# Down projection of a transformer block: six instead of five feature blocks by seven products, other homes for two operand sets, another order of blocks

## The chip, the core and the metric

The kernel runs on one core of a Trainium2 chip. Its time is the device time of one execution in microseconds. Before the change it takes 769.16 us (median of 3 runs, 768.88 to 769.38).

## The reference

One layer of an encoder: a token mixer (two attention groups), cross-attention into 256 memory tokens, and a SwiGLU feed-forward network, each between two RMS norms, on 512 tokens of width 1024, all in float32. The change lies in the last product, `@ w_down`, of the feed-forward network:

```python
D_MODEL = 1024
SEQ = 512
D_FF = -(-8 * D_MODEL // 768) * 256          # 2816

def swiglu(h, w_gate_up, w_down):
    g, u = jnp.split(h @ w_gate_up, 2, axis=-1)
    return (jax.nn.silu(g) * u) @ w_down

    ...
    h = rms_norm(x, g_ffn_pre[l])
    x = x + rms_norm(swiglu(h, w_gate_up[l], w_down[l]), g_ffn_post[l])
```

## The kernel before

Every float32 operand is held as two parts, a rounded high part and the remainder as a low part, and a product is three matmuls: high by high, high by low, low by high (`mm3`, lines 143, 144 and 146). ScalarE (ACT) makes the high part by a cast, VectorE (DVE) the low part by a subtraction. So each new operand costs both engines a pass.

**The down projection.** The hidden layer has 2816 features, 11 blocks (0 to 10) of 256. The output is made in two halves of 512 columns. For each half the loop at the end of the kernel goes through the feature blocks in the order of `DOWN[half]` and adds each block's product into the four accumulators of the half, one for each tile of 128 tokens. The last two blocks of half 0, and the last three of half 1, are `ends`: they are taken tile by tile, so that a tile is ready before the next one begins.

A *plain* block is 4 tiles x 2 x 3 = 24 matmuls of 512 columns (`down`). The blocks in `SEVEN` are computed by Winograd's form of Strassen's method instead: tokens, features and columns are each split in two, and the 2 x 2 by 2 x 2 block product takes seven products of half size instead of eight (`seven_products`). That is 7 x 2 x 3 = 42 matmuls of 256 columns. Four of the products go to banks of their own (p1, p5, p6, p7) that sum over all such blocks, and `gather` adds them up behind the last one.

A seven-product block needs two things that a plain one doesn't:

- An *operand set* of the hidden features: seven pieces of 128 x 256, four of them the blocks themselves and three made of sums, each as a high and a low part. `late_seven(u)` makes the set of block u: ACT casts pieces of 256, 512 and 1024 columns, and DVE subtracts as many and makes four sums of 256 (lines 1306 to 1309). The set is made once, in half 0, and used in both halves. Its home is two buffers, one for the high and one for the low parts: "latex" for blocks 4 and 5 (tags x1 and x2), "latehi" and "latelo" for 6 and 7.
- Weights of which four 256-column pieces are sums. `seven_down` makes them as two entries of the ring: a first one of three pieces as they are (lines 1001 and 1002, 256 and 512 columns), then three sums on DVE (lines 1007 to 1009, 512, 256 and 256 columns) and a second entry of 1024 columns (lines 922 and 923).

**The weight ring** has four places of 1024 columns, for high and low parts. A plain block takes one place, a seven-product block two. `take` starts as many fills as places are free; a place is free when PE has done with the entry four earlier. The raw weights come by DMA from the SyncE queue into three buffers (`fraw`), each of which is loaded again when DVE has subtracted from it for the last time.

**When the sets are made.** While half 0 works on blocks 0, 1, 2 and 3 (all plain), the sets of 4, 5, 6 and 7 are made. Behind block 4's products those of the last two stored blocks follow: block 9 is split whole into a high and a low part (`late`, for a plain product) in the buffer "latev" (tag vm), and block 8, copied first to "f8", gets a set in what is left of "latev" and in "latep" (tag pt). The buffers of tags vm and pt held the hidden blocks 1 to 7 and 8 to 9 until then, so they come free with the last reader of those.

Here the order on each engine is set by a scheduler from the program order and its priorities; each engine then works strictly in that order.

Of the kernel before, what the change touches and what calls it, by code (L numbers as in the profile page):

```python
# [8 lines left out]
F32 = mybir.dt.float32  # L9
F32R = mybir.dt.float32r  # L10
AF = mybir.ActivationFunctionType
ALU = mybir.AluOpType
AX = mybir.AxisListType

P = 128
# [17 lines left out]
AS_WEIGHTS, AS_MOVING = 16, 48  # L33
# [3 lines left out]
def hybrid_block_kernel(  # L37
# [20 lines left out]
    act, dve, pool, pe = nc.scalar, nc.vector, nc.gpsimd, nc.tensor  # L58
# [12 lines left out]
    def f32(ap):  # L71
        return ap.bitcast(F32)
# [119 lines left out]
    def bcast(g):  # L192
        return bass.AP(g.tensor, g.offset, [[0, P], [1, D]])
# [11 lines left out]
    for side in range(2):  # L205
        for g in fox_order if side == 0 else (0, 1):
            c = (0, 1544)[side] + 256 * g
            n = 264 if (side, g) == (0, 1) else 256
# [20 lines left out]
    ox = ctx.enter_context(tc.tile_pool(name="ox", bufs=1))  # L229

    with tc.tile_pool(name="mix", bufs=1, reuse_waits="tile") as bp:
# [126 lines left out]
        for t in range(NT):  # L358
# [3 lines left out]
                out=z[:, t, :], in0=acc0[t][:, 256:264], scalar=r, in1=gn[:, B_F : B_F + 8],  # L362
# [34 lines left out]
        for b in range(3):  # L397
            l = bp.tile([P, 2, SEQ], F32R, tag=f"L{b}", name=f"L{b}")
# [209 lines left out]
        for n, (side, g) in enumerate(order):  # L608
            with later(-20):
                q, kt, kl, v = group_proj(f"{side}{g}")  # L610
            if n == 3:
# [4 lines left out]
                for k in range(0, KB, 2):  # L616
                    b = msq[:, 2 * (k > 0) : 2 * (k > 0) + 2, :]
# [44 lines left out]
    with tc.tile_pool(name="cross", bufs=1, reuse_waits="tile") as cp:  # L662
        vm = cp.tile([P, 2 * 2 * D + 64], F32R, tag="vm", name="vm")
        vm = vm[:, : 2 * 2 * D].rearrange("p (s t n) -> p s t n", s=2, t=2)
        pt = cp.tile([P, 2 * 2 * SEQ + 64], F32R, tag="pt", name="pt")
        pt = pt[:, : 2 * 2 * SEQ].rearrange("p (s k n) -> p s k n", s=2, k=2)
# [16 lines left out]
        with later(-115):  # L683
            for c in range(4):
                hi, lo = unit()
                acc = bank("a")
                for b in range(2):
# [9 lines left out]
                    out=kT[:, 1, 2 * c : 2 * c + 2, :], in0=a3,  # L697
                    in1=f32(kT[:, 0, 2 * c : 2 * c + 2, :]), op=ALU.subtract,
# [7 lines left out]
        for half in range(2):  # L706
            hi, lo = unit()
            for t in range(NT):
                acc = bank("a")
                for k in range(4):  # L710
# [5 lines left out]
                    out=m, in0=acc, scalar=rs_g[1][:, t : t + 1], in1=m, op0=ALU.mult, op1=ALU.add  # L716
# [3 lines left out]
                if half:  # L720
                    r = small(1, "prs")
                    dve.scalar_tensor_tensor(
                        out=r, in0=mix_ms[:, 0, t : t + 1], scalar=EPS, in1=mix_ms[:, 1, t : t + 1],
# [4 lines left out]
                        out=mix[:, t, :], in0=mix[:, t, :], scalar=r, in1=xo[t], op0=ALU.mult, op1=ALU.add  # L728
# [39 lines left out]
        for h in range(4):  # L768
            hi, lo = unit()
            q = qq[:, h % 2]  # L770
            for b in range(2):
                acc = bank("a")
                cs = slice(b * P, (b + 1) * P)
                for k in range(KB):
# [3 lines left out]
                    out=q[:, 1, b, :], in0=acc, scalar=1.0 / 16.0, in1=f32(q[:, 0, b, :]),  # L778
                    op0=ALU.mult, op1=ALU.subtract,
                )  # L780
            p = cp.tile([P, NT, NMEM], F32, tag="xp", name=f"xp{h}", bufs=2)
            for i in range(0, NT, 2):
                s = bank("s")
                for j in range(2):
# [8 lines left out]
                    out=nm, in_=s.rearrange("p (j n) -> p j n", j=2), axis=AX.X, op=ALU.max, negate=True  # L793
# [9 lines left out]
                for j in range(2):  # L803
                    dve.tensor_scalar(
                        out=p[:, i + j, :], in0=p[:, i + j, :], scalar1=rs[:, j : j + 1],
# [11 lines left out]
            for b in range(2):  # L817
                acc = bank("o")
                cs = slice((2 * h + b) * P, (2 * h + b + 1) * P)
                for k in range(2):  # L820
# [6 lines left out]
                    out=oTl[2 * h + b], in0=acc, in1=f32(oTh[2 * h + b]), op=ALU.subtract  # L827
# [150 lines left out]
        def item(at, size, fill):  # L978
            items.append((at, at + size, fill))

        SEVEN = (4, 5, 6, 7, 8)
        DOWN = ((0, 1, 2, 3, 4, 5, 6, 7, 8, 9, 10), (0, 4, 5, 6, 7, 8, 1, 2, 3, 9, 10))
        dslot = [0]

        def down_slot():
            dslot[0] += 1
            return 1024 * ((dslot[0] - 1) % 4)
# [27 lines left out]
        for half in range(2):  # L1015
            for i in DOWN[half]:
                if i in SEVEN:
                    seven_down(i, half)
                    continue
                at = down_slot()  # L1020
# [33 lines left out]
        gh, gl, gf = {}, {}, []  # L1054
# [31 lines left out]
        gf_views = {}  # L1086
# [24 lines left out]
        for pair in range(2):  # L1111
            ns = slice(pair * 256, (pair + 1) * 256)
# [173 lines left out]
        def room(p, tag, n, bufs=1):  # L1286
            t = p.tile([P, n + 16], F32R, tag=tag, name=f"late{tag}", bufs=bufs)
            return t[:, 16 : 16 + n].rearrange("p (c n) -> p c n", n=256)

        x1, x2 = (room(ox, tag, 14 * 256) for tag in ("x1", "x2"))  # L1290
        late7 = [(x1[:, 0:7], x1[:, 7:14]), (x2[:, 0:7], x2[:, 7:14])]
        late7 += [tuple(room(wp, tag, 7 * 256, 2) for _ in range(2)) for tag in ("hi", "lo")]
        late7 = dict(zip(SEVEN, late7))

        def late_seven(u):

            h, l = late7[u]
            f = gf_views[u].rearrange("p (c n) -> p c n", n=256)

            def put(d, a):  # L1300
                act.copy(h[:, d], f[:, a])
                dve.tensor_tensor(out=l[:, d], in0=f[:, a], in1=f32(h[:, d]), op=ALU.subtract)

            put(slice(0, 1), slice(0, 1))
            put(slice(1, 3), slice(2, 4))
            dve.tensor_tensor(out=f[:, 3], in0=f[:, 1], in1=f[:, 3], op=ALU.add)
            dve.tensor_tensor(out=f[:, 1], in0=f[:, 0], in1=f[:, 1], op=ALU.subtract)
            dve.tensor_tensor(out=f[:, 0], in0=f[:, 3], in1=f[:, 0], op=ALU.subtract)
            dve.tensor_tensor(out=f[:, 2], in0=f[:, 2], in1=f[:, 0], op=ALU.subtract)
            put(slice(3, 7), slice(0, 4))  # L1310

        def late(u, flat):
            h, l = (flat[:, i * 1024 : (i + 1) * 1024] for i in range(2))
            act.copy(h, gf_views[u])
            dve.tensor_tensor(out=l, in0=gf_views[u], in1=f32(h), op=ALU.subtract)
            for b in range(2):
                gh[2 * u + b] = h[:, b * 512 : (b + 1) * 512]
                gl[2 * u + b] = l[:, b * 512 : (b + 1) * 512]

        yd = big.tile([P, NT, D], F32, tag="sB", name="yd")  # L1320

# [11 lines left out]
        for half, tail in enumerate((2, 3)):  # L1333
# [31 lines left out]
            def block(dst, u, a, w, c, end=False):  # L1365
                for n in range(2):
                    to = slice(n * 256, (n + 1) * 256)
                    b = dst
                    if isinstance(dst, tuple):
                        b, to = accs[dst[0] + n], (left, right)[dst[1]]  # L1370
                    lhs = [x[:, a, n * P : (n + 1) * P] for x in late7[u]]
                    mm(b, to, lhs, (w[0][:, c], w[1][:, c]), end and n == 1)

            def seven_products(u, last):
# [21 lines left out]

            body = DOWN[half][: FB // 2 - tail]
            for i in body:
                if i in SEVEN:
                    if half == 0 and i == SEVEN[0]:  # L1400
                        cuts.append(P)
                    seven_products(i, i == SEVEN[-1])
                    if half == 0 and i == SEVEN[0]:
                        spare = cp.tile([P, 4160], F32R, tag="vm", name="latev")
                        copied = cp.tile([P, 1024], F32, tag="xp", name="f8", bufs=2)
                        act.copy(copied, gf_views[8])
                        gf_views[8] = copied
                        late(9, spare)
                        at = 2048 + AS_WEIGHTS
                        lows = cp.tile([P, 2112], F32R, tag="pt", name="latep")[:, AS_WEIGHTS:]  # L1410
                        late7[8] = tuple(
                            a.rearrange("p (c n) -> p c n", n=256) for a in (spare[:, at : at + 1792], lows[:, :1792])
                        )
                        late_seven(8)
                        gb3 = cp.tile([P, D], F32, tag="xp", name="gb3", bufs=2)
                        spare3 = cp.tile([P, D], F32, tag="xp", name="spare3", bufs=2)
                        junk3, gained = spare3[:, :512], spare3[:, 512:]
                        nc.gpsimd.dma_start(gb3, bcast(g_ffn_post))
                    if i == SEVEN[-1]:
                        gather()  # L1420
                    continue
                (w,) = take()
                if half == 0 and i < 4:
                    late_seven(SEVEN[i])
                for t in range(NT):
                    if half and t == NT - 1 and DOWN[1].index(i) + 1 == DOWN[1].index(SEVEN[0]):
                        cuts.append(384)
                    down(t, i, w, half == 1 and t == NT - 1 and i == body[-1])
                    if held and t == 1:
                        cur.p3()  # L1430
                        held.clear()
                        cur.op2()
                        cur.mult(0)
                        keep(cur.u, cur.dst)
            ends = take(tail)
            for t in range(NT):
                yt = yd[:, t, cs]
                if half and t == NT - 1:
# [3 lines left out]
                    for n, (to, b) in enumerate(((left, bank("a")), (right, bank("a")))):  # L1442
                        for j, w in enumerate(ends):
                            down(t, DOWN[half][FB // 2 - tail + j], w, j == tail - 1, (to,), b)
                        dve.tensor_tensor(out=yt[:, to], in0=b[:, to], in1=yt[:, to], op=ALU.add)
# [7 lines left out]
                for j, w in enumerate(ends):  # L1453
                    down(t, DOWN[half][FB // 2 - tail + j], w, j == tail - 1)
                if half == 0:
# [68 lines left out]
```

## Time and profile before

| | before |
|---|---|
| median of 3 runs | 769.16 us |
| the profiled execution | 769.24 us, of which the profile's span is 767.5 us |
| instructions | 12862 |
| plain 512-column matmul, mean (L143, ps_a with g) | 390 ns, pipelined |
| fp32r low part of 1024 columns on DVE (L923 from fraw) | 1.20 us mean over 26 |
| weight loads of 512 KB (`fraw`), issue to landing | 3.5 us median |
| HBM read, written | 77.13 MB, 2.10 MB |

The page gives each engine's busy time; matmuls are pipelined, so the durations in a timeline overlap and the distance of two starts is what one costs. The feed-forward network lies behind some 440 us of the span, the down projection behind 645 us: half 0 to about 703 us, half 1 to 760 us. In square brackets behind a row stands the idle time of the engine ahead of it and what ended that.

### The profile page before, as it was taken

The page shows a single profiled execution, that of the slowest core. Times are in us where ns is not written, and L with a number is a line of the kernel's source. Part 1 is how long each engine was busy: PE and PEld are TensorE (multiplying, and loading weights), DVE is VectorE, ACT ScalarE, POOL GpSimd, SP SyncE. Part 2 cuts the span into 40 slices and gives each one's busy share as a digit, 9 for nine tenths or more (in the row PEclk, how much of TensorE's full clock was granted, in tenths as well). Part 3 has the DMA queues.
Part 4 walks back from the last instruction along what each step waited for, and adds up shares of the span by engine and source line. Part 5 has one row for each costly group of instructions (what it writes and reads, how often), then busy time and mean ns, then how long its engine had stood idle before and what let it go on. Part 6 is the DMA issues. An engine that isn't in the chain of part 4 may idle for free.

```text
span 767.5 us, 12862 instructions
## 1 busy us (share of the span) xinstructions
PE 752.7 (98%) x4988; PEld 674.4 (88%) x4988; DVE 595.7 (78%) x1083; ACT 442.9 (58%) x811; POOL 63.6 (8%) x105
## 2 busy tenths in 40 slices
PE   9999999999999999999999999999999999999996
PEld 9977888887778988877778899999999999898985
DVE  8667889789886688555653897999999999987746
ACT  7558889667875457444563635555555557543411
POOL 1001132100321201000001200000000000000001
PEclk9999999999999999999999999999999999999998
DMA  7522123422323735421341132333333323233312
GB/s 268 145 64 76 29 56 95 126 83 60 109 80 83 265 120 186 118 76 59 108 147 48 56 102 65 110 111 110 111 111 110 111 84 110 83 115 107 108 58 109
DMA packets 60748, 80.05 MB, mean 104 GB/s; under 512 B 2704, under 2 KB 43664, under 8 KB 60688
## 3 DMA queue, kind: packets, MB, share of 16 engines
q1 hardware_dynamic: 59264, 74.49, 30.9%
q0 software_dynamic: 1280, 4.72, 1.8%
q8 instruction: 39, 0.64, 0.4%
q14 instruction: 21, 0.17, 0.1%
q10 hardware_dynamic: 144, 0.02, 0.0%
HBM read 77.13 MB, written 2.10 MB: 103 GB/s over the span
## 4 chain that ended last, share of the span: by engine, by line
PE 87%; ACT 6%; DVE 4%; issue 2%; POOL 1%; DMA 1%; DVEq 0%; POOLq 0%; ACTq 0%
PE ps_a L144 13%; PE ps_a L146 13%; PE ps_a L143 13%; PE ps_t L1130 3%; PE ps_t L1127 3%; PE ps_s L1128 3%; PE ps_t L1128 3%; PE ps_s L1127 3%; PE ps_s L1130 3%; PE ps_s L143 2%; PE ps_s L146 2%; PE ps_s L144 2%; PE ps_t L552 2%; PE ps_o L561 2%; PE ps_s L533 1%
## 5 line engine op out<-in xcount | busy, mean ns | idle before, releaser
L126 DVE TENSOR_TENSOR lo<-raw,hi 128x1024 fp32r<-128x1024 f32 x56 | 68.2, 1223 | 20.6 <-ACT hi L125 20.4
L146 PE MATMUL ps_a<-hTh,lo 128*128 128x512 f32 x192 | 76.7, 399 | 0.0
L144 PE MATMUL ps_a<-hTl,hi 128*128 128x512 f32 x192 | 75.9, 395 | 0.0
L143 PE MATMUL ps_a<-hTh,hi 128*128 128x512 f32 x192 | 75.9, 395 | 0.0
L125 ACT CAST hi<-raw 128x1024 fp32r<-128x1024 f32 x56 | 57.8, 1047 | 25.5 <-PE ps_a L144 21.2
L923 DVE TENSOR_TENSOR ring_lo<-sums,ring_hi 128x1024 fp32r<-128x1024 f32 (+1 forms) x39 | 46.7, 1196 | 12.9 <-ACT ring_hi L922 8.5
L922 ACT CAST ring_hi<-sums 128x1024 fp32r<-128x1024 f32 (+1 forms) x39 | 40.1, 1029 | 17.2 <-PE ps_s L1128 15.6
L922 ACT CAST ring_hi<-fraw 128x1024 fp32r<-128x1024 f32 (+1 forms) x26 | 26.7, 1033 | 33.5 <-DVE fraw L1009 13.9
L923 DVE TENSOR_TENSOR ring_lo<-fraw,ring_hi 128x1024 fp32r<-128x1024 f32 (+1 forms) x26 | 31.0, 1201 | 14.2 <-ACT ring_hi L922 14.0
L144 PEld LDWEIGHTS ps_a<-hTl,hi 128*128 128x128 f32 x192 | 36.1, 188 | 6.4
L146 PEld LDWEIGHTS ps_a<-hTh,lo 128*128 128x128 f32 x192 | 36.1, 188 | 6.4
L143 PEld LDWEIGHTS ps_a<-hTh,hi 128*128 128x128 f32 x192 | 36.2, 188 | 5.6
L547 ACT ACTIVATE p<-p,nm 128x128 f32<-128x128 f32 (+1 forms) x64 | 36.1, 565 | 8.1 <-DVE nm L537 7.2
L554 ACT CAST pth<-ps_t 128x128 fp32r<-128x128 f32 (+1 forms) x64 | 27.0, 424 | 14.5 <-PE ps_t L552 13.7
L555 DVE TENSOR_TENSOR ptl<-ps_t,pth 128x128 fp32r<-128x128 f32 (+1 forms) x64 | 30.7, 487 | 5.0 <-ACT pth L554 3.7
L552 PE MATMUL ps_t<-ident,p 128*128 128x128 f32 x160 | 28.2, 275 | 1.1 <-DVE p L549 0.8
L549 DVE TENSOR_SCALAR p<-p,rc 128x128 f32<-128x128 f32 (+1 forms) x64 | 26.8, 418 | 0.1
L552 PEld LDWEIGHTS ps_t<-ident,p 128*128 128x128 f32 x160 | 19.3, 140 | 7.3 <-issue 2.4
L143 PE MATMUL ps_a<-hi,oh 128*128 128x512 f32 x64 | 25.5, 399 | 0.0
L1130 PE MATMUL ps_a<-b,ring_lo 128*128 128x256 f32 (+1 forms) x93 | 25.5, 276 | 0.0
L1127 PE MATMUL ps_a<-b,ring_hi 128*128 128x256 f32 x92 | 25.5, 277 | 0.0
L1128 PE MATMUL ps_a<-b,ring_hi 128*128 128x256 f32 x92 | 25.4, 276 | 0.0
(546 smaller groups left out, 2760.9 us busy)
## 6 DMA issues: line engine op xcount, KB each, us to landing
raw<-in_dram SPq DMA_DIRECT2D x64, 512.0 KB, 3.9
fraw<-in_dram SPq DMA_DIRECT2D x26, 512.0 KB, 3.5
place<-in_dram SPq DMA_DIRECT2D x21, 512.0 KB, 4.3
more_room<-in_dram SPq DMA_DIRECT2D x15, 512.0 KB, 4.3
cb<-in_dram SPq DMA_DIRECT2D x8, 256.0 KB, 2.7
xo<-in_dram POOLq DMA_DIRECT2D x4, 512.0 KB, 7.6
out_dram<-yd SPq DMA_DIRECT2D x8, 256.0 KB, 2.0
rawv<-in_dram SPq DMA_DIRECT2D x3, 520.0 KB, 6.3
```

The lines of the kernel that those rows point to most:

```text
L125: act.copy(hi[:, j : j + n, :], raw)
L126: dve.tensor_tensor(out=lo[:, j : j + n, :], in0=raw, in1=f32(hi[:, j : j + n, :]), op=ALU.subtract)
L143: pe.matmul(dst, sh, mh, start=first, stop=False)
L144: pe.matmul(dst, sh, ml, start=False, stop=False)
L146: pe.matmul(dst[:, to], sl, mh[:, to], start=False, stop=last)
L547: act.activation(p[:, :n], p[:, :n], AF.Exp, bias=nm, scale=-1.0, accum_out=sm)
L552: pe.transpose(tp[:, k * P : (k + 1) * P], p[:, k * P : (k + 1) * P], ident)
L922: act.copy(h2, v)
L923: dve.tensor_tensor(out=l2, in0=v, in1=f32(h2), op=ALU.subtract)
L1127: pe.matmul(dst, w[0][:, k, :], b[:, 0, k, :], start=first and k == 0, stop=False, skip_group_check=more)
L1128: pe.matmul(dst, w[0][:, k, :], b[:, 1, k, :], start=False, stop=False, skip_group_check=more)
L1130: pe.matmul(dst[:, to], w[1][:, k, :], b[:, 0, k, to], start=False, stop=last and k == 3, skip_group_check=more,)
```

## The change

- `SEVEN` gets block 9: six of the eleven blocks by seven products, five plain.
- The order of half 0 becomes 0, 1, 2, then 4 to 9 by seven products, then 3 and 10 as its ends (before: 0 to 3, 4 to 8, then 9 and 10). Half 1 becomes 0, 4 to 9, 1, then 2, 3 and 10 (before: 0, 4 to 8, 1, 2, then 3, 9 and 10).
- The set of block 7 is no longer made beside a plain block: behind the products of block 4 come the sets of 7 and then 8, behind those of block 5 the set of 9.
- Blocks 8 and 9 are both copied ("f8" and "f9"), and have new homes: block 8 all of "latevm" (tag vm), block 9 the high parts in "latept" (tag pt) and the seven low parts one by one: one in latept, two in latevm, two in small tiles "latev" and one each at the end of the two latex buffers. So its low parts are seven subtractions of 256 columns and not one each of 256, 512 and 1024.

```diff
-        SEVEN = (4, 5, 6, 7, 8)
-        DOWN = ((0, 1, 2, 3, 4, 5, 6, 7, 8, 9, 10), (0, 4, 5, 6, 7, 8, 1, 2, 3, 9, 10))
+        SEVEN = (4, 5, 6, 7, 8, 9)
+        DOWN = ((0, 1, 2, 4, 5, 6, 7, 8, 9, 3, 10), (0, 4, 5, 6, 7, 8, 9, 1, 2, 3, 10))
...
-        x1, x2 = (room(ox, tag, 14 * 256) for tag in ("x1", "x2"))
+        x1, x2 = (room(ox, tag, 15 * 256) for tag in ("x1", "x2"))
...
             def put(d, a):
                 act.copy(h[:, d], f[:, a])
-                dve.tensor_tensor(out=l[:, d], in0=f[:, a], in1=f32(h[:, d]), op=ALU.subtract)
+                if not isinstance(l, list):
+                    dve.tensor_tensor(out=l[:, d], in0=f[:, a], in1=f32(h[:, d]), op=ALU.subtract)
+                    return
+                for i in range(d.stop - d.start):
+                    dve.tensor_tensor(
+                        out=l[d.start + i], in0=f[:, a.start + i], in1=f32(h[:, d.start + i]), op=ALU.subtract
+                    )
...
-        def late(u, flat):
-            h, l = (flat[:, i * 1024 : (i + 1) * 1024] for i in range(2))
-            act.copy(h, gf_views[u])
-            dve.tensor_tensor(out=l, in0=gf_views[u], in1=f32(h), op=ALU.subtract)
...
+        def last_homes():
+            for u in (8, 9):
+                copied = cp.tile([P, 1024], F32, tag="xp", name=f"f{u}", bufs=2)
+                act.copy(copied, gf_views[u])
+                gf_views[u] = copied
+            vm, pt = (
+                cp.tile([P, AS_WEIGHTS + n * 256 + 48], F32R, tag=tag, name=f"late{tag}")[
+                    :, AS_WEIGHTS : AS_WEIGHTS + n * 256
+                ].rearrange("p (c n) -> p c n", n=256)
+                for tag, n in (("vm", 16), ("pt", 8))
+            )
+            v = [cp.tile([P, 256], F32R, tag="v", name="latev", bufs=2) for _ in range(2)]
+            lows = [pt[:, 7], vm[:, 14], vm[:, 15], *v, x1[:, 14], x2[:, 14]]
+            late7[8] = vm[:, 0:7], vm[:, 7:14]
+            late7[9] = pt[:, 0:7], lows
...
                     if half == 0 and i == SEVEN[0]:
-                        spare = cp.tile([P, 4160], F32R, tag="vm", name="latev")
-                        copied = cp.tile([P, 1024], F32, tag="xp", name="f8", bufs=2)
-                        act.copy(copied, gf_views[8])
-                        gf_views[8] = copied
-                        late(9, spare)
...
-                        late_seven(8)
+                        late_seven(SEVEN[3])
+                        last_homes()
+                    if half == 0 and i in SEVEN[:2]:
+                        late_seven(SEVEN[4 + SEVEN.index(i)])
+                    if half == 0 and i == SEVEN[1]:
                         gb3 = cp.tile([P, D], F32, tag="xp", name="gb3", bufs=2)
...
-                if half == 0 and i < 4:
+                if half == 0:
                     late_seven(SEVEN[i])
```

On PE, at the end of half 0's plain blocks, the order of the two programs differs like this (rows with - stand only before, with + only in the change; "g" are hidden blocks for a plain product, "latex" the set of block 4):

```order
-L143 MATMUL ps_o_7081<-ring_hi,g_5655 128x512
-L144 MATMUL ps_o_7081<-ring_lo,g_5655 128x512
-L146 MATMUL ps_o_7081<-ring_hi,g_5656 128x512
-L1349 MATMUL ps_s_7082<-ring_hi,latex_7070 128x256
-L1350 MATMUL ps_s_7082<-ring_lo,latex_7070 128x256
-L1352 MATMUL ps_s_7082<-ring_hi,latex_7070 128x128 x2
+L1363 MATMUL ps_s_7082<-ring_hi,latex_7070 128x256
+L1364 MATMUL ps_s_7082<-ring_lo,latex_7070 128x256
+L1366 MATMUL ps_s_7082<-ring_hi,latex_7070 128x128 x2
```

The rows with g are the end of block 3; in the change block 4 comes straight behind block 2, with the same cut matmul at its start.

On DVE, in half 0, before: from the second weight entry of block 6 (raw weights fraw_7289) to that of block 7 (fraw_7361); fraw_7414 is block 8, latep the low set of block 8:

```order
L923 TENSOR_TENSOR ring_lo<-fraw_7289,ring_hi 128x1024
L1302 TENSOR_TENSOR latep<-f_7320,latev 128x1024
L1002 TENSOR_TENSOR ring_lo<-fraw_7361,ring_hi 128x512
L1008 TENSOR_TENSOR fraw_7361<-fraw_7361 128x256
L1009 TENSOR_TENSOR fraw_7361<-fraw_7361 128x256
L1002 TENSOR_TENSOR ring_lo<-fraw_7414,ring_hi 128x256
L1007 TENSOR_TENSOR fraw_7414<-fraw_7414 128x512
L923 TENSOR_TENSOR ring_lo<-fraw_7361,ring_hi 128x1024
```

In the change 24 instructions stand between the second weight entry of block 6 (fraw_7251) and that of block 7 (fraw_7332). These are the last of them, with the entry itself; fraw_7402 is block 8, f_7291 and f_7293 are the copies of the hidden blocks 8 and 9:

```order
L1303 TENSOR_TENSOR latevm<-f_7291,latevm 128x1024
L1314 TENSOR_TENSOR f_7293<-f_7293 128x256
L1008 TENSOR_TENSOR fraw_7332<-fraw_7332 128x256
L1315 TENSOR_TENSOR f_7293<-f_7293 128x256
L1009 TENSOR_TENSOR fraw_7332<-fraw_7332 128x256
L1002 TENSOR_TENSOR ring_lo<-fraw_7402,ring_hi 128x256
L1002 TENSOR_TENSOR ring_lo<-fraw_7402,ring_hi 128x512
L1306 TENSOR_TENSOR latev<-f_7293,latept 128x256 x2
L1306 TENSOR_TENSOR latex_7070<-f_7293,latept 128x256
L1306 TENSOR_TENSOR latex_7071<-f_7293,latept 128x256
L923 TENSOR_TENSOR ring_lo<-fraw_7332,ring_hi 128x1024
```

Between the same two weight entries there stood one piece of one set before (block 8's large low part); now the sets of blocks 8 and 9 stand there nearly whole, and the second weight entry of block 7 comes behind the last piece of block 9's set.

Where the change moves the making of block 7's set, the DVE's order around block 5's second weight entry (fraw_7187) is this; latelo is block 7's set, latept the high part of block 9's:

```order
L1303 TENSOR_TENSOR latelo<-gf_4979,latelo 128x256
L1009 TENSOR_TENSOR fraw_7187<-fraw_7187 128x256
L1303 TENSOR_TENSOR latelo<-gf_4979,latelo 128x512
L1306 TENSOR_TENSOR latept<-f_7293,latept 128x256
L1312 TENSOR_TENSOR gf_4979<-gf_4979 128x256
L923 TENSOR_TENSOR ring_lo<-fraw_7187,ring_hi 128x1024
```

Before, block 7's first pieces stood ahead of block 4's second weight entry; now they stand just ahead of block 5's, mixed with the first piece of block 9's.

More of the change, by code (lines that the diff above doesn't have):

```diff
@@ L1310, in late_seven @@
             put(slice(3, 7), slice(0, 4))
-        def late(u, flat):
-            h, l = (flat[:, i * 1024 : (i + 1) * 1024] for i in range(2))
[L1314 to L1318, printed above, removed]
+        def last_homes():
[13 more added lines that the diff above has]
+            late7[9] = pt[:, 0:7], lows
         yd = big.tile([P, NT, D], F32, tag="sB", name="yd")
@@ L1370, in block @@
                         b, to = accs[dst[0] + n], (left, right)[dst[1]]
-                    lhs = [x[:, a, n * P : (n + 1) * P] for x in late7[u]]
+                    ns = slice(n * P, (n + 1) * P)
+                    lhs = [x[a][:, ns] if isinstance(x, list) else x[:, a, ns] for x in late7[u]]
                     mm(b, to, lhs, (w[0][:, c], w[1][:, c]), end and n == 1)
@@ L1403, in hybrid_block_kernel @@
                     if half == 0 and i == SEVEN[0]:
-                        spare = cp.tile([P, 4160], F32R, tag="vm", name="latev")
-                        copied = cp.tile([P, 1024], F32, tag="xp", name="f8", bufs=2)
-                        act.copy(copied, gf_views[8])
-                        gf_views[8] = copied
-                        late(9, spare)
[L1409 to L1413, printed above, removed]
-                        late_seven(8)
+                        late_seven(SEVEN[3])
[3 more added lines that the diff above has]
+                    if half == 0 and i == SEVEN[1]:
                         gb3 = cp.tile([P, D], F32, tag="xp", name="gb3", bufs=2)
```

## The prediction

> **What bounds the kernel now.** I read the page's busy shares first, then its chain of work that ended last, then the stretches of the down projection.
>
> ```profile
> PE 752.7 (98%) x4988; PEld 674.4 (88%) x4988; DVE 595.7 (78%) x1083; ACT 442.9 (58%) x811; POOL 63.6 (8%) x105
> ...
> PE 87%; ACT 6%; DVE 4%; issue 2%; POOL 1%; DMA 1%; DVEq 0%; POOLq 0%; ACTq 0%
> ```
>
> TensorE (PE) is busy 98% of the span and holds 87% of the chain, so a matmul less is time less, as long as nothing else comes late. Which engine would be late next depends on the stage. The stretches below are half 0's four plain blocks, its five seven-product blocks and its last two blocks; the columns are length, then busy time and instructions of PE, PEld, DVE, ACT and POOL, granted clock, DMA share and GB/s.
>
> ```profile
> 645.33:668.50 23.17, 23.17 (x111) 19.34 (x109) 22.84 (x41) 12.68 (x18) 0.57 (x1) 1.00 0.28 95
> 668.50:692.43 23.93, 23.93 (x213) 23.93 (x211) 19.18 (x30) 12.99 (x18) 0.00 (x0) 1.00 0.36 114
> 692.43:703.31 10.88, 10.88 (x50) 9.01 (x49) 9.09 (x16) 3.40 (x9) 0.00 (x0) 1.00 0.26 91
> ```
>
> PE never waits in them. But VectorE (DVE) is full in the first, 22.84 of 23.17 us: it makes both the low parts of the weights and the operand sets of the later seven-product blocks. It has 4.75 us to spare in the second. DVE is the engine one step behind the bound, and the change touches exactly its work.
>
> **The gain on PE.** The PE timeline, with start, duration and instruction, at the edges of blocks:
>
> ```profile
> 663.06 0.39 PE L143 MATMUL ps_a<-ring_hi,g 128*128 128x512 f32 x1
> 663.29 0.39 PE L144 MATMUL ps_a<-ring_lo,g 128*128 128x512 f32 x1
> ...
> 668.50 0.28 PE L1349 MATMUL ps_s<-ring_hi,latex 128*128 128x256 f32 x1
> ...
> 678.15 0.28 PE L143 MATMUL ps_s<-ring_hi,latehi 128*128 128x256 f32 x1
> 678.26 0.28 PE L144 MATMUL ps_s<-ring_lo,latehi 128*128 128x256 f32 x1
> ...
> 682.91 0.28 PE L143 MATMUL ps_s<-ring_hi,latelo 128*128 128x256 f32 x1
> ...
> 684.95 0.28 PE L143 MATMUL ps_s<-ring_hi,latelo 128*128 128x256 f32 x1
> ```
>
> Durations overlap, so starts count. Plain block 3 takes 663.06 to 668.50, 5.44 us for 24 matmuls of 512 columns; block 6 by seven products takes 678.15 to 682.91, 4.76 us for 42 of 256. Block 9 passes from the one kind to the other in both halves: 2 x 0.68 = **1.36 us** less. The cut matmul that stands at the first seven-product block of each half stays there, so it adds nothing.
>
> **What is moved, and the deadline that moves with it.** In half 0 block 3 goes behind the seven-product blocks. They start 5.44 us earlier. The row at 684.95 above is the first matmul of block 7's second weight piece (the four weight blocks that are sums); in the change PE wants that piece at 684.95 - 5.44 = **679.51 us**. What DVE has to do ahead of it grows at the same time: block 9's set is now seven pieces and three sums more instead of one plain subtraction.
>
> I lay out DVE's queue from the row at 643.91, the last with the same place in both orders, to the subtraction that completes block 7's second piece. DVE works strictly in program order, and its pitch is read from neighbours that do not wait:
>
> ```profile
> 641.17 0.42 DVE L1212 TENSOR_TENSOR U<-ps_a,U 128x256 f32<-128x256 f32 x1
> 641.51 1.22 DVE L923 TENSOR_TENSOR ring_lo<-fraw,ring_hi 128x1024 fp32r<-128x1024 f32 x1
> 642.64 0.42 DVE L1306 TENSOR_TENSOR gf<-gf 128x256 f32<-128x256 f32 x1
> 642.98 0.69 DVE L923 TENSOR_TENSOR ring_lo<-sums,ring_hi 128x512 fp32r<-128x512 f32 x1
> 643.58 0.42 DVE L1212 TENSOR_TENSOR G<-ps_a,rrow 128x256 f32<-128x256 f32 x1
> 643.91 0.42 DVE L1307 TENSOR_TENSOR gf<-gf 128x256 f32<-128x256 f32 x1
> ...
> 669.43 1.23 DVE L1315 TENSOR_TENSOR latev<-gf,latev 128x1024 fp32r<-128x1024 f32 x1 [1.12 <-ACT latev L1314]
> ...
> 682.25 1.23 DVE L923 TENSOR_TENSOR ring_lo<-fraw,ring_hi 128x1024 fp32r<-128x1024 f32 x1
> ```
>
> 256 columns take 0.335 us, 512 take 0.60, 1024 take 1.135. By the change's order 74 instructions stand between:
> - the last of the gate and up blocks: 2 of 256, 3 of 512, 1 of 1024 columns;
> - weights: block 2 (1 of 1024), blocks 4, 5 and 6 (each 3, 2, 1), block 7 without its last (3, 2) and the first pieces of block 8 (1, 1): 13, 9, 4;
> - operand sets: the rest of block 4 (2, 0, 1), blocks 5, 6, 7 and 8 (each 5, 1, 1), and block 9 with 7 pieces and 4 sums (11 of 256): 33, 4, 5.
>
> Together 48, 16 and 10: 48 x 0.335 + 16 x 0.60 + 10 x 1.135 = **37.03 us** of work from 644.25. Two waits join it, both for casts of ScalarE (ACT):
>
> ```profile
> 643.85 0.28 PE L1130 MATMUL ps_s<-b,ring_lo 128*128 128x256 f32 x1
> ...
> 642.65 0.92 ACT L1301 CAST latehi<-gf 128x256 fp32r<-128x256 f32 x2
> ...
> 665.68 1.05 ACT L1301 CAST latelo<-gf 128x1024 fp32r<-128x1024 f32 x1 [1.78 <-DVE gf L1309]
> ```
>
> The first: block 4's first subtraction is now second in the queue and needs a cast into ring space that PE reads until the row at 643.85; the cast can end near 644.5, a wait of 0.3. Queued behind it are the gate's last sums and block 4's set, which PE wants only at 663. The second: block 7's large subtraction needs its cast, which waits for the last sum (L1309), as the row at 665.68 does; only one weight sum stands between, so DVE waits some 0.9 us. So the subtraction starts near 644.25 + 37.03 + 0.3 + 0.9 = 682.5 and ends 1.23 later, at 683.7. PE stalls 683.7 - 679.5 = **4.2 us** there.
>
> The same list for before, as a test of the price: 38, 16 and 12 instructions make 35.95 us, and with the wait of 1.12 at 669.43 they give 681.3, while the row stands at 682.25; small gaps between dependent neighbours cost 0.9. That is my margin. No waits at all would give a stall of 3.0, both waits and those gaps 5.1. I take 4.3, nearer to the worked out waits than to the gaps, since dependent neighbours are mostly interleaved in the new order.
>
> Behind it, DVE needs 3.7 us more for the pieces of 8 and 9 until block 8's second piece (688.6); PE, 4.3 late, wants that at 684.27 + 4.3 = 688.6. So 0.1 us at most; block 9 and the last two blocks follow with slack, as block 3's own weights cost DVE one 1.135 for 5.44 us of PE.
>
> **What the stall itself triggers.** Two things on PE:
>
> ```profile
> 1.05 4.37 PE L241 MATMUL ps_t<-rrow 128*128 128x128 f32 x20 [1.05 <-DVE ones L80]
> ...
> 441.36 1.06 PE L170 MATMUL ps_t<-ident,y 128*128 128x128 f32 x8 [0.15 <-DVE f L181]
> ...
> 758.07 0.28 PE L144 MATMUL ps_a<-ring_lo,g 128*128 128x256 f32 x1
> 758.19 0.28 PE L146 MATMUL ps_a<-ring_hi,g 128*128 128x256 f32 x1
> ...
> 759.99 0.28 PE L146 MATMUL ps_a<-ring_hi,g 128*128 128x256 f32 x1
> ...
> 759.36:762.77 3.41, 0.91 (x8) 0.71 (x6) 2.39 (x8) 1.02 (x4) 0.54 (x1) 1.00 0.40 154
> 762.77:767.40 4.63, 0.00 (x0) 0.00 (x0) 1.33 (x2) 0.00 (x0) 0.00 (x0) 0.50 0.29 113
> ```
>
> The clock: after the last matmul (759.99 + 0.28) the granted clock is 0.50 from 762.77 on, 2.5 us later. A stall of 4.3 is longer. Coming back costs at most what the start shows: 20 passes in 4.37 us, 218 ns each, against 1.06/8 = 132 or less later, so some 4 us at half speed, 2.0 us lost; at least nothing, if the clock falls late or returns at once. I take 1.2, between them, as the clock falls somewhere inside the stall. [...]
>
> The pace: 256-column matmuls follow each other at 0.113 us (678.15 to 678.26), but at 0.12 in the last tile (758.07 to 758.19), where no matmul is cut to put them in step. If the restart loses the step, the 24 + 2 x 42 = 108 matmuls left of blocks 7 to 9 cost 108 x 0.0066 = 0.7 us. Nothing to 0.7; I take 0.35.
>
> **Edits at no cost.** ACT copies two blocks instead of one (L1406, one row below, 1.05 us) and has 10.5 us idle in 645.33:668.50. SyncE's queue keeps its order; the load for block 7 follows block 4's last weight subtraction near 656 and lands in the 3.5 us of the weight loads in the page, ahead of the ring space at 670. POOL's load of the gain row now waits for block 9's set (683) and is wanted near 700. In half 1 no set is made; there DVE is busy 3.70 of 5.00 us, so a sixth such block there is covered.
>
> ```profile
> 653.85 1.05 ACT L1406 COPY f<-gf 128x1024 f32<-128x1024 f32 x1
> ...
> 710.12:715.12 5.00, 5.00 (x47) 5.00 (x46) 3.70 (x6) 1.98 (x4) 0.00 (x0) 1.00 0.34 107
> ...
> fraw<-in_dram SPq DMA_DIRECT2D x26, 512.0 KB, 3.5
> ```
>
> **Sum.** -1.36 + 4.3 + 0.1 + 1.2 + 0.35 = +4.6 us on the profiled execution's own 769.24 us (span 767.5), which stands 0.08 above the median of 769.16: **773.8 us**.
>
> **Rivals.** *A: DVE keeps up.* All the seven-product pieces arrive in time, because PE's lead over DVE is less than I count; then only PE's saving stays, 769.24 - 1.36 = 767.9. For it: DVE has 4.75 us to spare in 668.50:692.43 of before. Against it: before had block 3's 5.44 us of cover ahead of that stretch, and 7's second piece had only 684.95 - 683.48 = 1.5 us of slack even so. It decides where DVE ends that piece by 679.5; 4.2 us must go. Chance 0.08. *B: a short stall*, 1 to 2.8 us, where the list is right but DVE's gaps and waits are fewer and work passes out of its way: 769 to 770.7, 0.07. *C: the stall without a clock fall*, because the clock needs longer idleness than 4.3 us to drop, or no longer than the restart to return: -1.36 + 4.3 + 0.1 + 0.35 gives 772.6, 0.22. [...] *D: all at its upper end*: 5.1, 0.1, 2.0 and 0.7 less 1.36 give 769.24 + 6.5 = 775.8 or more, 0.10. My forecast, stall with a partly slow restart: 0.53.
>
> **How the numbers follow.** The range takes C, the forecast and the nearer part of D: 771.4 to 775.6; 0.15 lies below with A and B, a little above. A measurement of this kernel can tell about 0.2%, 1.5 us, from no change. A's 767.9 is 0.16% under the median, so it counts as no change for the most part: faster 0.03, same 0.11 (most of A and B), slower 0.86.
>
> **What would show it.** Right: in the changed profile PE idles some 4 us near 679.5, once, at the first p5 matmul (set "latelo", block 7) with the release by DVE L923; DVE is without idle from 645 to 683; the granted clock dips in that slice; seven-product blocks of half 1 run at 4.76 us with no wait; half 0's other blocks sum to 0.68 less. Wrong: PE at full pace through 680, or DVE reaching block 7's second piece before 679.5; or PE waiting at another piece, which would mean that my list of the queue is sound and its order is not; or a stall of 4 us with the clock at 1.00 throughout (C).

## The result, and the profile after

| | before | after |
|---|---|---|
| median | 769.63 us (768.88 to 770.06, 17 runs) | 770.75 us (770.38 to 771.08, 17 runs) |
| ratio to before | 1 | 1.0015, 95% interval 1.0008 to 1.0022 |
| profiled execution, its span | 769.24 us, 767.5 us | 770.59 us, 768.8 us |

The three runs of before that stand ahead of the prediction are among its 17. The change makes the kernel 1.1 us slower. The direction was forecast, the size was not: 773.8 us, with a range from 771.4, stands above every run.

The page of after, busy shares and the chain that ended last:

```profile
PE 752.7 (98%) x5024; PEld 675.6 (88%) x5024; DVE 602.1 (78%) x1103; ACT 446.7 (58%) x818; POOL 63.6 (8%) x105
...
PE 81%; DVE 9%; ACT 6%; issue 2%; POOL 1%; DMA 1%; DVEq 0%; POOLq 0%; ACTq 0%
```

PE's share of the chain falls from 87% to 81% and DVE's rises from 4% to 9%: some work of DVE is now what PE waits for. The stretches of after tell where. They are half 0's three plain blocks; its first three seven-product blocks with the first weight entry of the fourth (block 7), up to where PE first falters; the piece with the waits; the rest of the seven-product blocks; the last two blocks; and half 1's six seven-product blocks; the columns are as in the prediction (length, busy time and instructions of PE, PEld, DVE, ACT and POOL, granted clock, DMA share, GB/s):

```profile
645.33:663.06 17.73, 17.73 (x86) 14.91 (x85) 17.73 (x33) 11.64 (x16) 0.00 (x0) 1.00 0.18 63
663.06:679.50 16.44, 16.44 (x146) 16.42 (x145) 15.65 (x33) 7.71 (x12) 0.10 (x1) 1.00 0.20 65
679.50:689.10 9.60, 8.10 (x65) 7.44 (x64) 9.53 (x19) 5.95 (x8) 0.47 (x1) 1.00 0.34 111
689.10:694.38 5.28, 5.28 (x48) 5.28 (x47) 2.86 (x4) 1.56 (x3) 0.00 (x0) 1.00 0.80 273
694.38:705.26 10.88, 10.88 (x50) 9.03 (x49) 8.98 (x16) 4.17 (x10) 0.00 (x0) 1.00 0.33 109
710.80:739.44 28.64, 28.64 (x253) 28.64 (x252) 19.65 (x29) 12.29 (x17) 0.00 (x0) 1.00 0.33 111
```

One stretch has PE short of work, the one that was forecast: from 679.50 PE is busy 8.10 of 9.60 us, DVE is full, and the granted clock stays at 1.00. Half 1 runs its six blocks in 28.64 us, 4.77 each, without a wait.

Without a wait half 0's six seven-product blocks would end at 663.06 + 0.12 (the cut matmul at their start) + 6 x 4.76 = 691.74; the next block starts at 694.38. So 2.64 us are lost. Less the gain of 1.36 that is +1.28, and the span grew by 768.8 - 767.5 = 1.3. **The whole question is why 2.6 us were lost there and not 5.95** (4.3 + 0.1 + 1.2 + 0.35 in the prediction's sum).

The PE timeline of after at that place (start, duration, instruction; in brackets the idle time ahead of it and what ended it):

```profile
679.42 0.28 PE L146 MATMUL ps_a<-ring_hi,latelo 128*128 128x256 f32 x1
679.53 0.28 PE L143 MATMUL ps_s<-ring_hi,latevm 128*128 128x256 f32 x1
680.45 0.39 PE L144 MATMUL ps_s<-ring_lo,latevm 128*128 128x256 f32 x1 [0.65 <-DVE ring_lo L1002]
680.67 0.28 PE L146 MATMUL ps_s<-ring_hi,latevm 128*128 128x256 f32 x1
681.81 0.39 PE L143 MATMUL ps_s<-ring_hi,latelo 128*128 128x256 f32 x1 [0.85 <-ACT ring_hi L922]
682.03 0.41 PE L143 MATMUL ps_t<-ring_hi,latelo 128*128 128x256 f32 x2
682.27 0.28 PE L143 MATMUL ps_a<-ring_hi,latelo 128*128 128x256 f32 x1
682.38 0.28 PE L143 MATMUL ps_o<-ring_hi,latelo 128*128 128x256 f32 x1
682.50 0.28 PE L143 MATMUL ps_s<-ring_hi,latevm 128*128 128x256 f32 x1
...
683.52 0.28 PE L143 MATMUL ps_a<-ring_hi,latevm 128*128 128x256 f32 x1
683.63 0.28 PE L144 MATMUL ps_s<-ring_lo,latelo 128*128 128x256 f32 x1
```

Block 7's first entry ends with the row at 679.42, and by the order of the code its second entry ("latelo" into ps_s) comes next. Instead "latevm" comes next, block 8. PE then does the matmuls of block 7 that need only high parts, then more of block 8, and at 683.63, without a wait, the first one that needs the late subtraction. And DVE was as late as forecast; its timeline in after:

```profile
679.98 1.02 DVE L1002 TENSOR_TENSOR ring_lo<-fraw,ring_hi 128x256 fp32r<-128x256 f32 x2
680.91 0.76 DVE L1306 TENSOR_TENSOR latev<-f,latept 128x256 fp32r<-128x256 f32 x2
681.58 0.76 DVE L1306 TENSOR_TENSOR latex<-f,latept 128x256 fp32r<-128x256 f32 x2
682.25 1.22 DVE L923 TENSOR_TENSOR ring_lo<-fraw,ring_hi 128x1024 fp32r<-128x1024 f32 x1
```

Forecast 682.5, measured 682.25. So DVE's part of the prediction stands and PE's part fell. The order of PE's instructions in the program of after says the same; the numbers count its rows (ps_s_7083 is p5, latelo block 7, latevm block 8):

```
4255 L143 MATMUL ps_a_7079<-ring_hi,latelo 128x256
4256 L144 MATMUL ps_a_7079<-ring_lo,latelo 128x256
4257 L146 MATMUL ps_a_7079<-ring_hi,latelo 128x256
4258 L143 MATMUL ps_s_7082<-ring_hi,latevm 128x256
4259 L144 MATMUL ps_s_7082<-ring_lo,latevm 128x256
4260 L146 MATMUL ps_s_7082<-ring_hi,latevm 128x256
4261 L143 MATMUL ps_s_7083<-ring_hi,latelo 128x256
4262 L143 MATMUL ps_t_7084<-ring_hi,latelo 128x256
4263 L143 MATMUL ps_t_7085<-ring_hi,latelo 128x256
...
4275 L143 MATMUL ps_a_7078<-ring_hi,latevm 128x256
4276 L144 MATMUL ps_s_7083<-ring_lo,latelo 128x256
```

Between the end of block 7's first entry (row 4257) and the first use of the late operand (row 4276) the code has one matmul, row 4261. Here 17 more stand there, 13 of block 8 and 4 high by high ones of block 7: at 0.113 us 1.9 us of work.

### The profile page after: what moved, and what is told of

Read it like the earlier page. It is cut to its first block, busy times and chain, and to the rows that moved or that the text cites. A ratio compares the mean times of both kernels' runs of the same rounds, so it can differ in the third digit from the quotient of the medians.

```text
span 768.8 us, 12965 instructions
## 1 busy us (share of the span) xinstructions
PE 752.7 (98%) x5024; PEld 675.6 (88%) x5024; DVE 602.1 (78%) x1103; ACT 446.7 (58%) x818; POOL 63.6 (8%) x105
## 4 chain that ended last, share of the span: by engine, by line
PE 81%; DVE 9%; ACT 6%; issue 2%; POOL 1%; DMA 1%; DVEq 0%; POOLq 0%; ACTq 0%
PE ps_a L144 12%; PE ps_a L146 12%; PE ps_a L143 12%; PE ps_t L1127 3%; PE ps_t L1130 3%; PE ps_t L1128 3%; PE ps_s L1128 3%; PE ps_s L1127 3%; PE ps_s L1130 3%; PE ps_s L143 2%; PE ps_s L144 2%; PE ps_s L146 2%; PE ps_t L552 2%; PE ps_o L561 2%; PE ps_s L533 1%
## 5 line engine op out<-in xcount | busy, mean ns | idle before, releaser
L923 DVE TENSOR_TENSOR ring_lo<-sums,ring_hi 128x1024 fp32r<-128x1024 f32 (+1 forms) x39 | 46.7, 1197 | 12.9 <-ACT ring_hi L922 8.5
L922 ACT CAST ring_hi<-sums 128x1024 fp32r<-128x1024 f32 (+1 forms) x39 | 40.2, 1030 | 17.2 <-PE ps_s L1128 15.6
L922 ACT CAST ring_hi<-fraw 128x1024 fp32r<-128x1024 f32 (+1 forms) x26 | 26.5, 1031 | 31.5 <-DVE fraw L1009 17.9
L923 DVE TENSOR_TENSOR ring_lo<-fraw,ring_hi 128x1024 fp32r<-128x1024 f32 (+1 forms) x26 | 30.8, 1200 | 11.7 <-ACT ring_hi L922 11.7
```

Of the source, the lines that this page charges most:

```text
L922: act.copy(h2, v)
L923: dve.tensor_tensor(out=l2, in0=v, in1=f32(h2), op=ALU.subtract)
```

## The experiments

**TensorE held to the order of the code** (e1_strict). Theory Q: what the prediction priced is right for PE in the order of the code, and the re-ordering is what saved the rest. Rival R: the re-ordering changes nothing, PE would have waited no longer anyway.

```diff
-        for half, tail in enumerate((2, 3)):
-            c0 = half * 512
+        with tc.manual_schedule(engines={mybir.EngineType.PE}):
+            for half, tail in enumerate((2, 3)):
+                c0 = half * 512
...
```

> The changed kernel with TensorE's matmuls of the down projection kept in the order of the code, so that block 8's first products no longer stand between block 7's. VectorE's queue stays the same up to block 7's second weight piece. Theory Q (VectorE ends that piece at 683.5 whatever TensorE does; the changed kernel lost only 2.6 us because TensorE had other matmuls in front of it): TensorE waits some 4.0 us between 679.5 and 683.6, and the time is 1.4 to 1.6 us above the changed kernel, about 772.2; if the idle stretch also halves the clock, 773 to 774. Theory R (the order of TensorE is of no account, 2.6 us is all that VectorE is late): as the changed kernel, 770.7.

774.53 us (773.9 to 775.39, 5 runs), 1.0063 times before (1.0050 to 1.0075). PE's timeline in this run, which entered the down projection 0.7 us later than after did (its first matmul there starts at 646.01, in after at 645.30):

```profile
680.13 0.28 PE L146 MATMUL ps_a<-ring_hi,latelo 128*128 128x256 f32 x1
682.69 0.38 PE L143 MATMUL ps_s<-ring_hi,latelo 128*128 128x256 f32 x1 [2.28 <-ACT ring_hi L922]
684.41 0.39 PE L144 MATMUL ps_s<-ring_lo,latelo 128*128 128x256 f32 x1 [1.34 <-DVE ring_lo L923]
684.63 0.28 PE L146 MATMUL ps_s<-ring_hi,latelo 128*128 128x256 f32 x1
684.75 0.36 PE L143 MATMUL ps_s<-ring_hi,latelo 128*128 128x256 f32 x1
684.91 0.42 PE L144 MATMUL ps_s<-ring_lo,latelo 128*128 128x256 f32 x1
685.13 0.42 PE L146 MATMUL ps_s<-ring_hi,latelo 128*128 128x256 f32 x1
...
687.91 0.42 PE L143 MATMUL ps_a<-ring_hi,latelo 128*128 128x256 f32 x1
688.12 0.33 PE L144 MATMUL ps_a<-ring_lo,latelo 128*128 128x256 f32 x1
```

and its stretches around the stall:

```profile
680.20:684.60 4.40, 0.78 (x4) 0.39 (x4) 4.40 (x11) 2.82 (x4) 0.57 (x1) 1.00 0.39 119
684.60:688.30 3.70, 3.70 (x20) 3.70 (x20) 3.63 (x9) 1.04 (x1) 0.00 (x0) 0.54 0.41 142
688.30:698.30 10.00, 10.00 (x90) 10.00 (x89) 6.07 (x6) 5.10 (x6) 0.00 (x0) 1.00 0.54 178
```

Here is the forecast stall, at the forecast piece. ACT's cast releases its one high by high matmul at 682.69, and the forecast releaser, DVE's L923, ends it: from 680.13 PE gets one matmul in before 684.41. Less the 0.113 us that each matmul takes anyway, PE lost 2.45 + 1.61 + 0.11 = 4.17 us. Then the granted clock is 0.54 over 3.70 us and the matmuls follow each other at 0.21 us in place of 0.11; by their starts that costs 1.6 us. Behind it PE runs at 0.114 us again. In all half 0 lost 5.9 us here (4.17 + 1.6 + 0.1), where after lost 2.64. Q holds and R falls; the median lies 0.5 us above Q's upper figure of 774.

**The same hold on the kernel before** (e5_before_strict), as a control: the hold could be dear by itself.

> The kernel before, with TensorE held to the order of the code in the down projection: the control for the strict run of the change (774.53 us). Theory Q (in the strict run the change's lateness was 4.1 us of waits and 1.7 us at half clock, all of it the change's own): DVE has block 7's second piece 1.5 us ahead of its use here, so PE waits nowhere in half 0; the strict order itself costs at most what the start of the blocks moved in the other strict run, 646.01 - 645.30 = 0.7 us. Time 769.6 to 770.5 us, half 0's five seven-product blocks 23.92 us as before, no granted clock under 0.99 between 646 and 760. Rival (the strict order is dear by itself, at the gate's end and where PE has to pass from block to block): 771.5 us or more, with waits of PE in other places than block 7's second piece; then most of the strict run's excess is not the change's.

769.96 us (769.25 to 770.84, 11 runs), 1.0007 times before (0.9997 to 1.0016); PE waits nowhere in the down projection. The hold costs nothing that can be told. Against this control the change with PE in the order of the code costs 774.53 - 769.96 = 4.6 us, and the prediction's sum was +4.6. By the stretches it is 5.9 - 1.36 = 4.5. That the sums agree so closely is partly luck: the stall was 4.17 for 4.3, the half clock 1.6 for 1.2, the lost pace 0.1 for 0.35, and block 8's wait nothing for 0.1.

**Block 3 left as cover** (e2_cover). Six seven-product blocks and the new homes stay, but block 3 keeps its place ahead of them, and block 7's set is made beside it again. Half 0 then ends with block 10 alone.

```diff
-        DOWN = ((0, 1, 2, 4, 5, 6, 7, 8, 9, 3, 10), (0, 4, 5, 6, 7, 8, 9, 1, 2, 3, 10))
+        DOWN = ((0, 1, 2, 3, 4, 5, 6, 7, 8, 9, 10), (0, 4, 5, 6, 7, 8, 9, 1, 2, 3, 10))
...
-        for half, tail in enumerate((2, 3)):
+        for half, tail in enumerate((1, 3)):
...
-                        late_seven(SEVEN[3])
                         last_homes()
```

> Six blocks by seven products and the new homes as in the changed kernel, but block 3 back ahead of the seven-product blocks (half 0 in the order 0 to 10, one block taken tile by tile at its end instead of two) and block 7's set made beside it. Theory Q (what cost 2.6 us was the 5.44 us of TensorE work that VectorE lost as cover): block 7's second piece ends near 684.5 and is wanted at 684.95, so no wait or one under 0.5 us; the time is before less 1.36 us, 767.9 to 768.4. Theory S (the set of block 9 with its 11 small instructions is what VectorE cannot carry): some 2 us of waiting stay, 769.9 or more.

768.64 us (768.39 to 769.32, 11 runs), 0.9986 times before (0.9977 to 0.9995); the counted gain of 1.36 us, 0.9982, lies in the interval. The stretch of its six seven-product blocks in half 0:

```profile
669.11:697.87 28.76, 28.76 (x254) 28.75 (x253) 25.28 (x46) 14.62 (x22) 0.57 (x1) 1.00 0.39 129
```

28.76 = 0.12 + 6 x 4.76 + 0.08: no wait. DVE's timeline has the subtraction of block 7's second entry here:

```profile
683.11 1.22 DVE L923 TENSOR_TENSOR ring_lo<-fraw,ring_hi 128x1024 fp32r<-128x1024 f32 x1
```

DVE ends that entry at 684.33, about when it does in after (683.47, in a time base 0.6 us earlier); what differs is that PE comes for it 5.44 us later. So a sixth seven-product block is worth its 1.36 us, block 9's scattered set included, and the loss of the change comes with the moved block 3 (and the set of block 7, which moves with it).

**The covered version held to the order of the code** (e6_cover_strict): it could be that this version, too, lives from the re-ordering.

> The covered version (six seven-product blocks, block 3 left in its place, the set of block 7 beside it; 768.64 us) with TensorE held to the order of the code. Theory Q (with block 3 in its place DVE ends block 7's second piece at 684.33, ahead of its use at 684.95 + 0.6, so PE needs no other work to fill a wait): its distance to the strict kernel before is that of the free versions, -1.0 us or -1.36 by count, and PE has no wait over 0.3 us in half 0: 768.3 to 769.5 us. Rival (the covered version too lives from the re-ordering of PE): PE waits of 0.5 us and more at the second pieces of blocks 7 to 9, and the time is that of the strict kernel before or above, 769.6 to 771.

768.43 us (767.85 to 769.03, 11 runs), 0.9985 times before (0.9976 to 0.9994), and no wait of PE in the down projection. It doesn't. The faster version needs no help from the scheduler; only the late one does.

**Block 3 moved, block 9 left plain** (e4_order5). The other half of the change, made in the kernel before: five seven-product blocks, block 3 behind them, block 7's set behind block 4's products.

```diff
-        DOWN = ((0, 1, 2, 3, 4, 5, 6, 7, 8, 9, 10), (0, 4, 5, 6, 7, 8, 1, 2, 3, 9, 10))
+        DOWN = ((0, 1, 2, 4, 5, 6, 7, 8, 3, 9, 10), (0, 4, 5, 6, 7, 8, 1, 2, 3, 9, 10))
...
+                        late_seven(SEVEN[3])
                         spare = cp.tile([P, 4160], F32R, tag="vm", name="latev")
...
-                if half == 0 and i < 4:
+                if half == 0 and i < 3:
                     late_seven(SEVEN[i])
```

> The kernel before, five blocks by seven products and the old homes, with only block 3 moved behind the seven-product blocks of half 0 (order 0, 1, 2, 4 to 8, 3, 9, 10) and the set of block 7 made behind block 4's products. No matmul is saved. Theory Q: the deadlines come 5.44 us earlier and VectorE saves only the 1.135 us of block 3's weights ahead of them; block 7's second piece ends near 681.8 against 679.5, and the time is 2.0 to 2.6 us above before, 771.2 to 771.8. Theory S (block 9's set and its new homes are the cost): as before, 769.2.

770.43 us (769.93 to 770.86, 11 runs), 1.0006 times before (0.9997 to 1.0014): no difference that can be told, and Q's two microseconds missed. DVE's timeline says why:

```profile
678.69 0.69 DVE L1002 TENSOR_TENSOR ring_lo<-fraw,ring_hi 128x512 fp32r<-128x512 f32 x1
679.29 1.22 DVE L923 TENSOR_TENSOR ring_lo<-fraw,ring_hi 128x1024 fp32r<-128x1024 f32 x1
680.43 1.22 DVE L1302 TENSOR_TENSOR latep<-f,latev 128x1024 fp32r<-128x1024 f32 x1
681.56 0.69 DVE L1007 TENSOR_TENSOR fraw<-fraw 128x512 f32<-128x512 f32 x1
```

Block 7's second entry (the 1.22 at 679.29) comes ahead of block 8's large piece (L1302) and of the 512-column sum (L1007); in before's order, from which I had counted, both stood ahead of it. That is 1.135 + 0.60 us that DVE no longer has in the way. Half 0 lost 0.59 us (block 3 starts at 688.30, without a wait 663.79 + 0.12 + 5 x 4.76 = 687.71). I had again taken an order for fixed, this time DVE's. PE runs block 7 in the order of the code here (its second entry begins at 680.24, straight behind the first), so no other matmuls hide a wait. What the run does show: moving block 3 without block 9's set uses up the lead and little more.

**Block 9's set begun one block later** (e3_late9): behind block 6's products and not behind block 5's, so that its pieces no longer stand ahead of block 7's second entry.

```diff
-                    if half == 0 and i in SEVEN[:2]:
-                        late_seven(SEVEN[4 + SEVEN.index(i)])
+                    if half == 0 and i in SEVEN[:3:2]:
+                        late_seven(SEVEN[4 + SEVEN.index(i) // 2])
```

> The changed kernel, with the set of block 9 begun behind block 6's products and not behind block 5's; nothing else differs in the code. Nine instructions of 256 columns, 3.0 us, leave the queue ahead of block 7's second weight piece. Theory Q: that piece ends at 680.7, the wait on it falls to about 1.2 us, and block 8's and 9's second pieces are up to 0.2 us late each; the time is 769.1 to 769.6, about the time before. Theory W (VectorE's total work up to block 9 is the bound, not its order): the wait only moves to blocks 8 and 9 and the time stays near 770.6.

771.38 us (770.89 to 772.04, 11 runs), 1.0022 times before (1.0013 to 1.0031): not better than the change, and some 2 us above Q's 769.1 to 769.6. PE loses about 1.0 us at block 7's second entry, as Q had it, and 0.25 at block 8's, but 1.5 more turned up at block 9's. PE's timeline there:

```profile
691.06 0.38 PE L143 MATMUL ps_s<-ring_hi,latept 128*128 128x256 f32 x1
692.32 0.39 PE L144 MATMUL ps_s<-ring_lo,latept 128*128 128x256 f32 x1 [0.88 <-DVE ring_lo L923]
```

PE gets one matmul in within 1.5 us. What DVE does ahead of that, in its timeline:

```profile
688.31 1.22 DVE L923 TENSOR_TENSOR ring_lo<-fraw,ring_hi 128x1024 fp32r<-128x1024 f32 x1
689.45 0.42 DVE L1009 TENSOR_TENSOR fraw<-fraw 128x256 f32<-128x256 f32 x1
691.04 2.42 DVE L923 TENSOR_TENSOR ring_lo<-fraw,ring_hi 128x1024 fp32r<-128x1024 f32 x2 [1.17 <-ACT ring_hi L922]
```

The row at 688.31 is block 3's weight, wanted only behind block 9, and it stands ahead of block 9's last weight sum (689.45). The sum, ACT's cast and the subtraction then follow each other with nothing beside them: DVE idles 1.17 us for the cast while PE waits for DVE. PE lost 2.9 us in half 0 in all (block 3 starts at 695.12, without a wait 692.24). The rival that the wait only moves is nearer.

## Why the prediction was right in sign and wrong in size

- **The gain of 1.36 us** was right. Half 1 shows 4.77 us a block with no wait, and the covered version shows it in the time, 0.9986 (0.9977 to 0.9995).
- **DVE's queue** was right: subtraction forecast at 682.5, measured 682.25. Of the two waits in it the second was 0.79 for 0.9; of the first 0.3 only some 0.1 came. The test of the price on before was a little better than it should have been: between the rows at 643.91 and 682.25 stand 37 instructions of 256 columns, not 38, so the gaps there come to 1.27 us and not 0.9. In after, whose list of 48, 16 and 10 is right, they come to 0.1.
- **The stall of 4.3 us was the step that failed.** It set DVE's lateness equal to PE's idleness: "PE stalls 683.7 - 679.5". That holds for PE in the order of the code, and there it measured 4.17 (e1_strict). But the scheduler orders PE too. I laid out DVE's order of the changed kernel row by row and took PE's from the code. In after PE found 17 other matmuls, 1.9 us, to do first, and 4.2 - 1.9 leaves 2.3; the timeline shows 2.06, two waits, (680.45 - 679.53) - 0.11 = 0.81 and (681.81 - 680.67) - 0.11 = 1.03, with 0.11 for each restart. The rest of the 2.64 are small waits between 686 and 689 and some matmuls at 0.12 us.
- **The clock term of 1.2 us** did not come: in after no idle stretch there was longer than 1.03 us, and the granted clock stayed 1.00. Where the stall did come it cost 1.6. The prediction took the fall from the end of before, where the granted clock is 0.50 from 762.77 on, 2.5 us behind the end of the last matmul. In the strict run no idle stretch was longer than 2.45 us, and the clock fell all the same. That delay is no fixed one: at the end of after the last matmul ends at 761.34 + 0.28 = 761.62, and the clock stays at 1.00 for 4.9 us behind it:

```profile
761.62:766.40 4.78, 0.00 (x1) 0.00 (x0) 2.84 (x7) 1.01 (x4) 0.54 (x1) 1.00 0.39 151
766.60:768.80 2.20, 0.00 (x0) 0.00 (x0) 0.00 (x0) 0.00 (x0) 0.00 (x0) 0.50 0.19 71
```

- **The lost pace of 0.35 us** was too much where it applied: 0.114 us after the restart in the strict run, against 0.113, makes 0.1 over the 88 matmuls. Nor does it take a cut matmul to come back to that pace: in after it goes from 0.12 (683.63 to 684.23) to 0.113 (684.23 to 686.16) with none between.
- **What releases PE** in after is no longer the large subtraction but DVE's L1002 for block 8 and ACT's cast L922 for block 7. The prediction had "PE waiting at another piece" as a sign that the list is sound and its order is not; it was PE's order. ACT's cast starts late, at 680.71: ahead of it on ACT stands a cast of block 9's set, which waits 1.85 us, until 679.76, for DVE:

```profile
679.76 1.05 ACT L1301 CAST latept<-f 128x1024 fp32r<-128x1024 f32 x1 [1.85 <-DVE f L1315]
680.71 1.04 ACT L922 CAST ring_hi<-fraw 128x1024 fp32r<-128x1024 f32 x1
```

- **Where the lateness comes from**: neither part makes it alone. The moved block 3 without the added set lost 0.6 us (e4_order5), the added set without the move nothing (e2_cover); together they lost 2.6 with PE's order left to the scheduler, and 5.9 with PE in the order of the code. The set's 11 instructions of 256 columns (3.7 us by the pitch, in place of one of 1.135) go onto a queue whose lead the move of block 3 has just used up.
- **Rival B** had a place for this: a stall of 1 to 2.8 us, 769 to 770.7. It got 0.07, because I looked for its reason on DVE, where work would have had to pass out of the way. The reason was on PE.

Open is how much of the 2.6 us hangs on ACT's queue (block 9's cast ahead of block 7's) and how much on DVE's: e3_late9 moved both at once. The trace of after bounds ACT's part at block 7's cast: the last weight sum that the cast needs ends on DVE at 679.64 + 0.42 = 680.06, and the cast starts at 680.71, so block 9's cast held it by 0.65 us at most. A version that takes away only one of them wasn't tried.

The version that beats both kernels is e2_cover: 768.64 us, or 0.9986 times before.

## What to carry to other kernels

Where a scheduler orders all engines, as here, a late operand costs its lateness less the work that the scheduler has put ahead of it on the waiting engine (4.2 us less 1.9 here); so list the waiting engine's order around the late operand, and not only the late engine's. Cover is counted in the time at which the operand is wanted: moving 5.44 us of plain matmuls from ahead of a full DVE queue to behind it cost 0.6 us while the queue's lead nearly covered it (e4_order5), and 2.6 once block 9's set stood in that queue as well. When several casts and subtractions feed one piece, moving one set later can put another piece's chain in the open, as it did here at block 9, where PE lost 1.5 us (e3_late9).

## What the hardware showed unexpectedly

The clock fell to half after two idle stretches of 2.45 and 1.61 us with one matmul between them (e1_strict, granted clock 0.54 in the 3.70 us behind them), and came back some 3.4 us later (684.75 to 688.12). In after two stretches of 0.81 and 1.03 us with two matmuls between them left it at 1.00. So one matmul in between was not enough to keep the clock there. What sets these cases apart, no run shows.
